# Hybrid decoder layer: raw output weights in token places, norm weights loaded in the last block, output tile and probabilities in pools by use, row diagonals ahead of sums

## The chip, the core and the metric

The kernel runs on one core of one Trainium2 chip. What is measured is the device time of one execution in microseconds. Before the change three runs took 1560.19, 1560.9 and 1562.3 us, a median of 1560.9. The program is written in Bass and Tile: each engine (TensorE or PE, VectorE or DVE, ScalarE or ACT, GpSimd or POOL, SyncE or SP, which issues most DMAs) has its own queue of instructions and works it off in order; semaphores tie the queues together.

## The reference

One step of a decoder layer on 4096 new prompt tokens and 64 sampled tokens, all in float32. `h @ w_in` is one projection to 2816 columns; three groups of heads use its columns, and their outputs go through one output projection:

```python
h = _rmsnorm(x, g_pre)
z = h @ w_in
cb, cc, ch, cg, q, k, v, ag, mq, mg = _split_cols(z)
...
out_a = jax.nn.silu(cg) * cb * conv                      # gated short convolution
o_b = _window_prompt(q, k, v, sink_g)                    # window of 128, 8 query heads, 2 key heads, sinks
out_b = jax.nn.silu(ag) * o_b
o_c = _mem_attend(mq.reshape(n, t, MEM_HEADS, HEAD_DIM), mem_k, mem_v)   # 4 heads over 256 memory tokens
out_c = jax.nn.silu(mg) * o_c
y = jnp.concatenate([out_a, out_b, out_c], axis=-1) @ w_out
return x + _rmsnorm(y, g_post), new_conv, new_k, new_v
```

The sampled tokens attend to cached keys and values instead. Besides the two outputs, the new keys, values and convolution states are returned.

## The kernel before

**Two halves.** The first half (`input_projection` and, for its first two blocks of tokens, `plain_block`) computes z for 8 blocks of 520 tokens each. It does so in three phases (`PHASES`), each for a part of the columns. Inside a phase, a block is made in seven products (`PRODUCTS`; a step is one product, `p` = 0 to 6) after Strassen's scheme, each in float32 as three passes over a high and a low part: `split` and `w_split` copy a tensor to its rounded high part on ACT and subtract to get the low part on DVE. The second half, attention and the output projection, runs over 33 blocks of 128 tokens (`Block`) and over 16 chunks of 256 tokens (`Chunk`).

**The last block of the third phase** (`ph == 2`, `b == last`) also prepares the second half: during its steps `wo_load` brings the 16 raw tiles of the output weights, 128x512 each (j = 0 to 15; j below 8 is the first half of the output columns), and `wo_split` splits each two steps later into a tile of the pool "wa". The raw tiles are taken from the pool "work" (tag "u"), which has five buffers: the sixth raw tile waits until the first has been split. "wa" has 21 buffers, which in this phase hold the weights of the seven products; each becomes free when its product is done. "hx" holds the four x tiles of the products; the last x is loaded three steps ahead, so its places become free during the last steps. When the last block is done, its z parts are split into zh and a remainder (`finish_parts`, L400 and L402) and stored to the DRAM tensor qd.

**The opening of attention.** `open_attention` closes the pools of the first half and opens those of the second in the same memory; a new tile that lies over an old one has to wait for the old one's last reader. Before the change, pool "wp" has the window probabilities (tags "sm", "pt", "pv"), "xp" those of the memory heads ("p", "xpt"), and "yp" on the other side holds the input rows xr, the output tile yn and one mix buffer. Then chunk 1's gates are loaded (`load_mix`), the rows of blocks 0 and 1 (`Block.load`), and `gpost`, the norm weights, 512 KB as one row broadcast over 128 partitions. All of these are issued by SP, in this order, behind the stores to qd.

**The units.** A chunk has eight units: four of window attention and four of memory attention. `window_unit` makes scores on PE (L1205), copies half of them from PSUM (ACT, L1207), replaces masked ones by the other half (DVE, L1208), takes maxima and exponentials and normalises; later it transposes (PE, L1228) and masks (POOL, L1235 and L1238). `cross_unit` is alike, with L1141, L1145, L1150 (POOL) and L1156. Scores of all units share two PSUM banks, transposes another two. `Pipe` starts a unit at given places of the output products (L1432): eight in each of the first two blocks, which therefore carry a whole chunk each, four in each later block. So while block 0's output is computed, chunk 1's units run. `Block.run` multiplies each half of the output by gpost (L1439), squares it (L1440), and adds the row (L1450). `Block.split` (L1412, L1413) splits the mixed heads of the next block.

**The order of instructions.** The first phase is written out by hand (`plain_jobs` and a manual schedule). From the second phase on a scheduler orders each engine's queue by estimated times, with a few instructions pinned by `keep_in_program_order`; so a change of a buffer or of a load's place also changes the order of what follows.

**The row factors.** RMSNorm of x needs a factor for each token. For block 2 of the first phase `rows_diag` writes five diagonal tiles of 104x104 (DVE, L291), `rows_product` multiplies them with ones (PE, L300), which spreads the factors over all partitions. `plain_jobs` lists in which step of which block this and the sums of weights (`first_sums`) are done.

Of the kernel before, what the change touches and what calls it, by code (L numbers as in the profile page):

```python
# [8 lines left out]
F32 = mybir.dt.float32  # L9
# [3 lines left out]
ALU = mybir.AluOpType  # L13
# [38 lines left out]
def hybrid_layer(ctx: ExitStack, tc: tile.TileContext, a: dict):  # L52
# [240 lines left out]
    def rows_bank(b):  # L293
        rows[b] = accumulator(1, 2, f"rows_y{b}")[:, :, :HW]
# [322 lines left out]
    def plain_jobs(b, s):  # L617

        gains = lambda b, *os: [lambda o=o: x_gain(0, b, o) for o in os]
        scales = lambda b, *os: [lambda o=o: x_scale(0, b, o) for o in os]  # L620
        parts = lambda b, o: [lambda: x_split(b, o)]
        fill = lambda o: [lambda q=q: first_fill(o, q) for q in range(4)]
        sums = lambda q, k: [lambda: first_sums(q, k)]
        fills = lambda q, *os: [lambda o=o: first_fills(q, o) for o in os]
        done = lambda b, row: finish(0, b, zz[b], row)
        row = [row_step]
        return {
            (0, 0): lambda: [*fill("A11"), *parts(0, "B21")],
            (0, 1): lambda: fill("A22"),
            (0, 2): lambda: [*fill("A12"), *parts(0, "B12"), *row],  # L630
            (0, 3): lambda: [*sums(0, 0), *row, *sums(0, 1), *fills(0, "S2"), *row],
            (0, 4): lambda: [*parts(0, "B22"), *fills(0, "S3", "S1"), *row, *fills(0, "S4"), *row],
            (0, 5): lambda: [*sums(1, 0), *row, *sums(1, 1), *fills(1, "S2", "S3"), *row],
            (0, 6): lambda: [*parts(1, "B11"), *row, *fills(1, "S1", "S4"), *sums(3, 0), *row],
            (0, 7): lambda: [*row, *fills(3, "S2", "S3"), lambda: rows_diag()],
            (1, 0): lambda: [*parts(1, "B21"), *row, *row, lambda: rows_bank(0), lambda: rows_product(0), *z_rows(0, 1)],
            (1, 1): lambda: [*z_rows(0, 0), *done(0, 1), *row, *row],
            (1, 2): lambda: [*parts(1, "B12"), *done(0, 0), *fills(3, "S1"), *row],
            (1, 3): lambda: sums(2, 0),
            (1, 4): lambda: [*row, *parts(1, "B22"), *gains(2, "B11"), *sums(2, 1), lambda: rows_diag(), lambda: rows_bank(2),  # L640
                             *fills(2, "S2"), *row],
            (1, 5): lambda: [lambda: rows_product(2), *fills(2, "S3", "S1"), *gains(2, "B21"), *fills(2, "S4"), *row],
            (1, 6): lambda: [*scales(2, "B11"), *gains(2, "B12"), *scales(2, "B21", "B12"), *row],
            (1, 7): lambda: [lambda: h_split(0), *gains(2, "B22"), *scales(2, "B22"), lambda: t_sum(0, 2, "T1"), *row,
                             *z_rows(1, 1)],
        }[b, s]()
# [220 lines left out]
    def wo_load(j):  # L867
        h, k = divmod(j, KT)
        wo_raw[j] = third["work"].tile([P, 512], F32, tag="u", name=f"wor{j}")
        DMA.dma_start(wo_raw[j], a["w_out"][k][:, 512 * h : 512 * h + 512])  # L870

    def wo_split(j):
# [12 lines left out]
              (1, 0, 4): lambda: next_fills("S4"),  # L885
              (1, 0, 5): lambda: next_fills("A22")}

    def input_projection():
        for i, (ph, b, p) in enumerate(steps):
# [36 lines left out]
            if ph == 2 and b == last:  # L926
                for j in ((0, 1, 2), (3, 4), (5, 6, 7), (8, 9), (10, 11, 12), (13, 14, 15), ())[p]:
                    jobs.append(lambda j=j: wo_load(j))
                    pending.setdefault(i + 2, []).append(lambda j=j: wo_split(j))
                if p == 4:  # L930
                    jobs.append(blocks[0].split)
# [35 lines left out]
    def open_attention():  # L967

        nonlocal ps, mixp, wp, xp, vp, bp, bq, yp
        own.close()  # L970
# [8 lines left out]
        bq = att.enter_context(tc.tile_pool(name="bq", bufs=1))  # L979
        wp = att.enter_context(tc.tile_pool(name="wp", bufs=2))  # L980
        xp = att.enter_context(tc.tile_pool(name="xp", bufs=2))
        bp = att.enter_context(tc.tile_pool(name="bp", bufs=1))
# [6 lines left out]

    ps = mixp = wp = xp = vp = bp = bq = yp = None  # L990
    att = ctx.enter_context(ExitStack())
# [8 lines left out]

    def work(pool, shape, tag, name, **kw):

        if ps is None:
            return third["work"].tile(shape, F32, tag="u", name=name)
        return pool.tile(shape, F32, tag=tag, name=name, **kw)

# [42 lines left out]
    class Chunk:  # L1049
# [83 lines left out]
        def cross_unit(self, h, pts):  # L1133
            c, nb = self.c, CT // P
            q = self.q[:, h]
            p = work(xp, [P, nb, 256], "p", f"xp{c}_{h}")
            mx, nm, den, rd = (tiny.tile([P, 4], F32, tag=n, name=f"x{n}{c}_{h}") for n in ("mx", "nm", "den", "rd"))
# [13 lines left out]
            yield 1  # L1151
            pt = work(xp, [P, 2, CT], "xpt", f"xpt{c}_{h}")
            for kt in range(2):
# [42 lines left out]
        def window_unit(self, i, kvh, steps):  # L1196
            b = 2 * self.c + i
            first = b == 0
            sm = work(wp, [P, 4, P], "sm", f"sm{b}_{kvh}")
            for half in range(2):  # L1200
# [26 lines left out]
            for hh in range(4):  # L1227
                TE.transpose(t[:, hh * P : (hh + 1) * P], sm[:, hh, :], ident)  # L1228
            pt = work(wp, [P, 512], "pt", f"wpt{b}_{kvh}")
            S.copy(pt, t)  # L1230
            p3 = pt.rearrange("p (h q) -> p h q", h=4)
            if not first:

                pv = work(wp, [P, 512], "pv", f"wpv{b}_{kvh}")
# [78 lines left out]
    def sample_window():  # L1313
# [20 lines left out]
        transpose_to(vn, [(zs[:, 5, :], 64)], "svnt")  # L1334
        sms = [wp.tile([P, 4, P], F32, tag="sm", name=f"ssm{half}").rearrange("p a n -> p (a n)")[:, : 2 * 192] for half in range(2)]
        sms = [t.rearrange("p (a n) -> p a n", a=2) for t in sms]
# [28 lines left out]
        yield  # L1365
        pt = wp.tile([P, 512], F32, tag="pt", name="swpt")
        transpose_to(pt, [(sm[i][:, 0:P], P) for i in range(4)], "swt0")
        ptn = wp.tile([P, 512], F32, tag="pv", name="swptn")[:64]
        transpose_to(ptn, [(sm[i][:, P:192], 64) for i in range(4)], "swt1")
# [19 lines left out]
    class Block:  # L1389
# [70 lines left out]
    blocks[1].load()  # L1460
    gpost = wa.tile([P, 2, 512], F32, tag="w", name="gpost").rearrange("p a n -> p (a n)")
    DMA.dma_start(gpost, a["gpost"].partition_broadcast(P))

# [158 lines left out]
```

## Time and profile before

| | us |
|---|---|
| median of three runs | 1560.9 |
| profiled execution, whole | 1560.18 |
| its span, from the first to the last instruction | 1558.4 |
| PE busy in the span | 1538.1 |
| mean granted PE clock | 0.996 of full |
| scores of chunk 1's first window unit on PE | from 941.6 |

A row of a timeline has the start and the length in us, the engine, the line of the kernel, the operation, the tiles as out<-in with the shape, and the number of instructions; brackets give how long the engine had been idle before it and what ended the wait. SPq is the queue of SP, which only issues DMAs; the length is that of the issue and not of the transfer. Matmuls overlap their neighbours by their pipeline, so a row's length is more than the step from one to the next. In the table of stages each engine has its busy time and its number of instructions, then comes the granted share of PE's clock, the mean busy share of the 16 DMA engines and the rate in GB/s.

### The profile page before, as it was taken

The page shows a single profiled execution, that of the slowest core. Times are in us where ns is not written, and L with a number is a line of the kernel's source. Part 1 is how long each engine was busy: PE and PEld are TensorE (multiplying, and loading weights), DVE is VectorE, ACT ScalarE, POOL GpSimd, SP SyncE. Part 2 cuts the span into 40 slices and gives each one's busy share as a digit, 9 for nine tenths or more (in the row PEclk, how much of TensorE's full clock was granted, in tenths as well). Part 3 has the DMA queues.
Part 4 walks back from the last instruction along what each step waited for, and adds up shares of the span by engine and source line. Part 5 has one row for each costly group of instructions (what it writes and reads, how often), then busy time and mean ns, then how long its engine had stood idle before and what let it go on. Part 6 is the DMA issues. An engine that isn't in the chain of part 4 may idle for free.

```text
span 1558.4 us, 30165 instructions
## 1 busy us (share of the span) xinstructions
PE 1538.1 (99%) x11341; PEld 1411.4 (91%) x11341; DVE 1155.2 (74%) x2075; ACT 796.3 (51%) x2031; POOL 380.7 (24%) x603
## 2 busy tenths in 40 slices
PE   9999999999999999999999998999999999999998
PEld 9999999999999999999999996788888888887876
DVE  6779888898988777986777677776666666666643
ACT  6776566575222222445454355666655655655632
POOL 0323232211300000010012103544444444444310
PEclk9999999999999999999999999999999999999999
DMA  9979999877755333679666969888777777777332
GB/s 265 199 206 260 249 277 269 291 237 259 191 178 178 124 124 124 245 225 311 231 223 196 278 219 279 166 171 157 164 149 159 146 147 158 152 160 154 122 109 95
DMA packets 175110, 305.59 MB, mean 196 GB/s; under 512 B 31093, under 2 KB 104821, under 8 KB 174933
## 3 DMA queue, kind: packets, MB, share of 16 engines
q1 hardware_dynamic: 128069, 226.69, 47.0%
q0 software_dynamic: 46176, 75.92, 25.5%
q8 instruction: 90, 1.47, 0.4%
q10 hardware_dynamic: 720, 1.05, 0.2%
q14 instruction: 55, 0.45, 0.1%
HBM read 196.54 MB, written 108.05 MB: 195 GB/s over the span
## 4 chain that ended last, share of the span: by engine, by line
PE 86%; DVE 4%; DMA 4%; issue 3%; ACT 1%; POOL 1%; SPq 0%; DVEq 0%; ACTq 0%; POOLq 0%
PE c L359 48%; PE y L1432 22%; PE ws L1205 3%; PE wo L1047 2%; PE wt L1228 2%; PE xs L1141 2%; PE xt L1156 2%; PE wo L1177 2%; PE wo L1183 1%; PE mem_acc L772 1%; DMA gpost<-in_gpost 1%; DMA wor<-in_w_out 1%; DMA vd<-v 0%; DVE z L366 0%; DMA rb<-rowd 0%
## 5 line engine op out<-in xcount | busy, mean ns | idle before, releaser
L1432 PE MATMUL y<-wo,mh 128*128 128x512 f32 (+1 forms) x1040 | 350.3, 400 | 0.0
L366 DVE TENSOR_TENSOR z<-c,z 128x520 f32<-128x520 f32 (+1 forms) x308 | 194.7, 645 | 90.8 <-PE c L359 89.5
L1432 PEld LDWEIGHTS y<-wo,mh 128*128 128x128 f32 x1040 | 194.3, 188 | 38.8 <-issue 2.0
L1432 PE MATMUL y<-wo,ml 128*128 128x512 f32 (+1 forms) x520 | 201.9, 388 | 0.0
L1218 ACT ACTIVATE sm<-sm,wnm 128x128 f32<-128x128 f32 x256 | 99.6, 391 | 70.7 <-DVE wnm L1212 70.7
L1150 POOL TENSOR_SCALAR xp<-xp,xrd 128x256 f32<-128x256 f32 x128 | 74.6, 589 | 192.2 <-DVE xrd L1146 192.1
L1432 PEld LDWEIGHTS y<-wo,ml 128*128 128x128 f32 x520 | 98.3, 189 | 16.2
L1142 DVE TENSOR_REDUCE xmx<-xs 128x2 f32<-128x512 f32 x64 | 44.1, 689 | 58.3 <-PE xs L1141 58.2
L1230 ACT COPY wpt<-wt 128x512 f32<-128x512 f32 x64 | 37.2, 582 | 86.2 <-PE wt L1228 86.2
L1205 PEld LDWEIGHTS ws<-kst,q 128*128 128x128 f32 x512 | 70.9, 193 | 10.2 <-issue 5.3
L1205 PE MATMUL ws<-kst,q 128*128 128x256 f32 x512 | 73.6, 285 | 4.9 <-issue 4.9
L1439 DVE TENSOR_TENSOR yn<-y,gpost 128x512 f32<-128x512 f32 (+1 forms) x66 | 45.1, 683 | 40.3 <-PE y L1432 39.2
L1440 ACT ACTIVATE y<-y 128x512 f32<-128x512 f32 (+1 forms) x66 | 38.5, 584 | 64.9 <-DVE yn L1439 64.9
L730 POOL CAST wmask<-negs 128x256 uint8<-128x256 f32 x1 | 1.4, 1372 | 267.9 <-DMA negs<-in_wmask 267.9
L1080 POOL DMA_DIRECT2D q<-qd x64 | 42.9, 676 | 97.4 <-DVE lo_7T L350 65.3
L1238 POOL TENSOR_SCALAR_AFFINE_SELECT wpt<-wpt 128x512 f32<-128x512 f32 x64 | 54.2, 848 | 48.3 <-ACT wpt L1230 45.4
L1145 ACT ACTIVATE xp<-xs,xnm 128x256 f32<-128x256 f32 x128 | 58.9, 464 | 4.4 <-DVE xnm L1143 4.2
L1069 POOL DMA_DIRECT2D kst<-qd x64 | 38.6, 619 | 83.1 <-PE xt L1156 42.0
L1235 POOL TENSOR_SCALAR_AFFINE_SELECT wpv<-wpt 128x512 f32<-128x512 f32 x62 | 40.4, 652 | 65.3 <-ACT wpt L1230 65.0
L1208 DVE COPY_PREDICATED sm<-wmask,ws 128x256 f32<-128x256 uint8 x124 | 52.3, 435 | 2.8 <-ACT sm L1207 2.6
L1450 DVE SCALAR_TENSOR_TENSOR xr<-yn,yst,xr 128x1024 f32<-128x1024 f32 (+2 forms) x34 | 43.5, 1282 | 13.5 <-POOL yst L1446 13.5
L1207 ACT COPY sm<-ws 128x256 f32<-128x256 f32 x128 | 44.8, 367 | 13.0 <-PE ws L1205 6.6
(962 smaller groups left out, 5119.5 us busy)
## 6 DMA issues: line engine op xcount, KB each, us to landing
q<-qd POOLq DMA_DIRECT2D x64, 384.0 KB, 7.7
xr<-in_x_p SPq DMA_DIRECT2D x32, 512.0 KB
nat<-in_x_p SPq DMA_DIRECT2D x39, 416.0 KB
o_yp<-xr SPq DMA_DIRECT2D x31, 512.0 KB
md<-th POOLq DMA_DIRECT2D x48, 260.0 KB, 6.5
qd<-zh SPq DMA_DIRECT2D x48, 260.0 KB
qd<-z SPq DMA_DIRECT2D x48, 260.0 KB
kst<-qd POOLq DMA_DIRECT2D x60, 192.0 KB, 5.8
```

Of the source, the lines that this page charges most:

```text
L359: TE.matmul(bank[:, :HW], l, r, start=first and i == 0, stop=last and i == 3 * KH - 1)
L366: add = lambda dst, other: V.tensor_tensor(dst, c, other, op=ALU.add)
L1142: V.tensor_reduce(mx[:, :nb], s, axis=AX.X, op=ALU.max)
L1145: S.activation(p[:, i, :], s[:, i, :], AF.Exp, bias=nm[:, i : i + 1], scale=SCALE, accum_out=den[:, i : i + 1])
L1150: G.tensor_scalar(p[:, i, :], p[:, i, :], rd[:, i : i + 1], 0.5, op0=ALU.mult, op1=ALU.mult)
L1205: TE.matmul(s3[:, hh, :], self.q[:, 4 + 2 * (2 * half + hh) + kvh, i * P : i * P + P], self.kst[:, 2 * kvh + part, i * P : i * P + 2 * P], ...
L1207: S.copy(sm[:, 2 * half : 2 * half + 2, :], s3[:, :, P : 2 * P])
L1208: V.copy_predicated(sm[:, 2 * half : 2 * half + 2, :], third["wmask"], third["negs"] if first else s3[:, :, 0:P])
L1218: S.activation(sm[:, hh, :], sm[:, hh, :], AF.Exp, bias=nm[:, hh : hh + 1], scale=SCALE, accum_out=den[:, hh : hh + 1])
L1238: G.affine_select(p3, p3, pattern=[[0, 4], [1, P]], compare_op=ALU.is_ge, fill=0.0, base=0, channel_multiplier=-1)
L1432: TE.matmul(acc, self.hl[l][:, k], wo[k][c0 // 512][:, r, c0 % 512 : c0 % 512 + c1 - c0], start=j == 0, stop=j == passes * KT - 1)
L1439: V.tensor_tensor(yn[:m, c0:c1], acc[:m], gpost[:m, c0:c1], op=ALU.mult)
```

## The change

Five things are done. Raw weights 10 to 13 go into two places of "hx", two to a place, and the loads of 10, 11 and 13 to 15 are issued one step earlier (the splits of 10 to 12 stay in the last step, p = 6, those of 13 to 15 move into it). `gpost` is loaded in step p = 2 of the last block, in a tile of "wa" as before. The probabilities and the output tile yn get a pool for each use ("sm", "p", "yn", "pt", "pv", "xpt"), all on the left side, with as many buffers as before; yn leaves "yp". In `plain_jobs` (1, 4), `rows_diag` and `rows_bank` come ahead of the split of B22, the gains and the second sum of weights. The instruction that negates the sink column of the sampled tokens is kept in program order.

```diff
-            (1, 4): lambda: [*row, *parts(1, "B22"), *gains(2, "B11"), *sums(2, 1), lambda: rows_diag(), lambda: rows_bank(2),
+            (1, 4): lambda: [*row, lambda: rows_diag(), lambda: rows_bank(2), *parts(1, "B22"), *gains(2, "B11"), *sums(2, 1),
                              *fills(2, "S2"), *row],
...
     def wo_load(j):
         h, k = divmod(j, KT)
-        wo_raw[j] = third["work"].tile([P, 512], F32, tag="u", name=f"wor{j}")
+        if 10 <= j < 14:
+
+            if j % 2 == 0:
+                third["raw"] = hxp.tile([P, KH, HW], F32, tag="hx", name=f"wor{j}").rearrange("p k n -> p (k n)")
+            wo_raw[j] = third["raw"][:, 512 * (j % 2) : 512 * (j % 2) + 512]
+        else:
+            wo_raw[j] = third["work"].tile([P, 512], F32, tag="u", name=f"wor{j}")
         DMA.dma_start(wo_raw[j], a["w_out"][k][:, 512 * h : 512 * h + 512])
...
+    def gains_load():
+        third["gpost"] = wa.tile([P, 2, 512], F32, tag="w", name="gpost").rearrange("p a n -> p (a n)")
+        DMA.dma_start(third["gpost"], a["gpost"].partition_broadcast(P))
...
-                for j in ((0, 1, 2), (3, 4), (5, 6, 7), (8, 9), (10, 11, 12), (13, 14, 15), ())[p]:
+                for j in ((0, 1, 2), (3, 4), (5, 6, 7), (8, 9, 10, 11), (12, 13, 14, 15), (), ())[p]:
                     jobs.append(lambda j=j: wo_load(j))
-                    pending.setdefault(i + 2, []).append(lambda j=j: wo_split(j))
+                    pending.setdefault(i + (3 if j in (10, 11) else 2), []).append(lambda j=j: wo_split(j))
+                if p == 1:
+                    pending.setdefault(i + 1, []).append(gains_load)
...
-        wp = att.enter_context(tc.tile_pool(name="wp", bufs=2))
-        xp = att.enter_context(tc.tile_pool(name="xp", bufs=2))
+        places = {tag: att.enter_context(tc.tile_pool(name=tag, bufs=1 if tag == "yn" else 2))
+                  for tag in ("sm", "p", "yn", "pt", "pv", "xpt")}
...
-    def work(pool, shape, tag, name, **kw):
+    def work(shape, tag, name):
 
         if ps is None:
             return third["work"].tile(shape, F32, tag="u", name=name)
-        return pool.tile(shape, F32, tag=tag, name=name, **kw)
+        return places[tag].tile(shape, F32, tag=tag, name=name)
...
-        V.tensor_scalar(scol[:, 1:2], scol[:, 0:1], -1.0, None, op0=ALU.mult)
+        tc.keep_in_program_order(V.tensor_scalar(scol[:, 1:2], scol[:, 0:1], -1.0, None, op0=ALU.mult))
...
-            yn = yp.tile([P, D], F32, tag="yn", name=f"yn{b}", bufs=1)
+            yn = work([P, D], "yn", f"yn{b}")
...
-    gpost = wa.tile([P, 2, 512], F32, tag="w", name="gpost").rearrange("p a n -> p (a n)")
-    DMA.dma_start(gpost, a["gpost"].partition_broadcast(P))
+    gpost = third["gpost"]
```

The other edits replace `work(wp, ...)`, `work(xp, ...)` and `wp.tile(...)` by `work(...)` with the tag.

More of the change, by code (lines that the diff above doesn't have):

```diff
@@ L967, in open_attention @@
     def open_attention():
-        nonlocal ps, mixp, wp, xp, vp, bp, bq, yp
+        nonlocal ps, mixp, places, vp, bp, bq, yp
         own.close()
@@ L988, in open_attention @@
         DMA.dma_start(third["scol"][:, 0:1], a["sinkcol"])
-    ps = mixp = wp = xp = vp = bp = bq = yp = None
+    ps = mixp = places = vp = bp = bq = yp = None
     att = ctx.enter_context(ExitStack())
@@ L1135, in cross_unit @@
             q = self.q[:, h]
-            p = work(xp, [P, nb, 256], "p", f"xp{c}_{h}")
+            p = work([P, nb, 256], "p", f"xp{c}_{h}")
             mx, nm, den, rd = (tiny.tile([P, 4], F32, tag=n, name=f"x{n}{c}_{h}") for n in ("mx", "nm", "den", "rd"))
@@ L1151, in cross_unit @@
             yield 1
-            pt = work(xp, [P, 2, CT], "xpt", f"xpt{c}_{h}")
+            pt = work([P, 2, CT], "xpt", f"xpt{c}_{h}")
             for kt in range(2):
@@ L1198, in window_unit @@
             first = b == 0
-            sm = work(wp, [P, 4, P], "sm", f"sm{b}_{kvh}")
+            sm = work([P, 4, P], "sm", f"sm{b}_{kvh}")
             for half in range(2):
@@ L1228, in window_unit @@
                 TE.transpose(t[:, hh * P : (hh + 1) * P], sm[:, hh, :], ident)
-            pt = work(wp, [P, 512], "pt", f"wpt{b}_{kvh}")
+            pt = work([P, 512], "pt", f"wpt{b}_{kvh}")
             S.copy(pt, t)
@@ L1232, in window_unit @@
             if not first:
-                pv = work(wp, [P, 512], "pv", f"wpv{b}_{kvh}")
+                pv = work([P, 512], "pv", f"wpv{b}_{kvh}")
                 G.affine_select(pv.rearrange("p (h q) -> p h q", h=4), p3, pattern=[[0, 4], [-1, P]], compare_op=ALU.is_gt,
@@ L1334, in sample_window @@
         transpose_to(vn, [(zs[:, 5, :], 64)], "svnt")
-        sms = [wp.tile([P, 4, P], F32, tag="sm", name=f"ssm{half}").rearrange("p a n -> p (a n)")[:, : 2 * 192] for half in range(2)]
+        sms = [work([P, 4, P], "sm", f"ssm{half}").rearrange("p a n -> p (a n)")[:, : 2 * 192] for half in range(2)]
         sms = [t.rearrange("p (a n) -> p a n", a=2) for t in sms]
@@ L1365, in sample_window @@
         yield
-        pt = wp.tile([P, 512], F32, tag="pt", name="swpt")
+        pt = work([P, 512], "pt", "swpt")
         transpose_to(pt, [(sm[i][:, 0:P], P) for i in range(4)], "swt0")
-        ptn = wp.tile([P, 512], F32, tag="pv", name="swptn")[:64]
+        ptn = work([P, 512], "pv", "swptn")[:64]
         transpose_to(ptn, [(sm[i][:, P:192], 64) for i in range(4)], "swt1")
```

## The prediction

> **What bounds the kernel now.** I read the page's busy times first, then the busy time by stage, then the timelines of the one stage that stands out. The page says TensorE:
>
> ```profile
> PE 1538.1 (99%) x11341; PEld 1411.4 (91%) x11341; DVE 1155.2 (74%) x2075; ACT 796.3 (51%) x2031; POOL 380.7 (24%) x603
> ```
>
> So at most 1558.4 - 1538.1 = 20.3 us of the span can be PE idling, and only a change to PE's idle time or to its clock can matter. The busy time by stage (start:end, then length, PE, PEld, DVE, ACT, POOL, granted PE clock, DMA share, GB/s) shows where. The projection ends and attention begins at about 941:
>
> ```profile
> 930.00:940.00 10.00, 10.00 (x86) 10.00 (x85) 10.00 (x16) 7.79 (x13) 2.56 (x4) 1.00 0.42 115
> 940.00:950.00 10.00, 8.44 (x48) 7.09 (x47) 5.26 (x9) 3.40 (x8) 0.08 (x1) 1.00 1.41 292
> 950.00:960.00 10.00, 6.61 (x30) 5.86 (x31) 8.10 (x22) 5.03 (x23) 1.60 (x3) 0.83 0.91 312
> 960.00:970.00 10.00, 8.43 (x54) 6.52 (x52) 6.94 (x18) 7.57 (x28) 8.69 (x16) 1.00 1.16 332
> 970.00:980.00 10.00, 8.94 (x47) 5.88 (x47) 6.21 (x20) 6.34 (x25) 2.13 (x5) 0.66 1.30 275
> 980.00:990.00 10.00, 9.60 (x66) 6.51 (x65) 8.23 (x23) 6.37 (x27) 5.27 (x9) 1.00 1.30 252
> 990.00:1000.00 10.00, 9.19 (x63) 7.75 (x64) 7.93 (x19) 7.03 (x25) 7.41 (x12) 1.00 0.41 103
> 1100.00:1200.00 100.00, 100.00 (x614) 82.06 (x613) 68.71 (x175) 58.85 (x220) 45.42 (x71) 1.00 0.76 155
> ```
>
> Before and after this passage PE is full; inside it PE idles and, in two slices, runs at a lower clock. PE's timeline names the gaps, in brackets with their releaser:
>
> ```profile
> 953.39 2.04 PE L1205 MATMUL ws<-kst,q 128*128 128x256 f32 x8 [4.95 <-issue]
> ...
> 968.52 0.98 PE L1156 MATMUL xt<-ident,xp 128*128 128x128 f32 x4 [1.30 <-issue]
> 971.14 1.54 PE L1047 MATMUL wo<-xpt,mkv 128*64 128x256 f32 x5 [1.06 <-DVE xpt L1160]
> ...
> 983.92 0.63 PE L1156 MATMUL xt<-ident,xp 128*128 128x128 f32 x4 [0.40 <-DVE xpt L1160]
> 993.00 0.33 PE L1156 MATMUL xt<-ident,xp 128*128 128x128 f32 x1 [0.81 <-POOL xp L1150]
> 998.24 0.63 PE L1141 MATMUL xs<-mk,q 128*128 128x256 f32 x4
> ```
>
> Idle: 4.95 + 1.30 + 1.06 + 0.40 + 0.81 = 8.5 us. Clock: 10 x (1 - 0.83) + 10 x (1 - 0.66) = 5.1 us of PE work not done. Together 13.6 us: **the ceiling** for anything done to this passage. The last row is my mark: from the scores at 998.24 on, the instructions stand in the same order on every compute engine in both programs (but for one of 128x1), so whatever is gained by then stays, and nothing later changes.
>
> **Why PE stops at 948.** The score product at 953.39 needs a PSUM bank that DVE must first read (the predicated copy, L1208, behind ACT's copy, L1207). The queues of SP, POOL, ACT and DVE in turn:
>
> ```profile
> 931.80 0.93 SPq L870 DMA_DIRECT2D wor<-in_w_out  x2
> 934.22 0.33 SPq L870 DMA_DIRECT2D wor<-in_w_out  x1
> 939.92 0.48 SPq L870 DMA_DIRECT2D wor<-in_w_out  x1
> ...
> 937.45 2.64 POOL L1080 DMA_DIRECT2D q<-qd  x4 [65.29 <-DVE lo_7T L350]
> ...
> 936.76 0.62 ACT L178 CAST wo<-wor 128x512 fp32r<-128x512 f32 x1 [0.44 <-DMA wor<-in_w_out]
> 947.54 0.62 ACT L178 CAST wo<-wor 128x512 fp32r<-128x512 f32 x1 [3.12 <-DMA wor<-in_w_out]
> 949.77 0.62 ACT L178 CAST wo<-wor 128x512 fp32r<-128x512 f32 x1 [0.28 <-DMA wor<-in_w_out]
> ...
> 948.20 0.69 DVE L182 TENSOR_TENSOR wo<-wor,wo 128x512 fp32r<-128x512 f32 x1 [3.58 <-ACT wo L178]
> 950.42 0.69 DVE L182 TENSOR_TENSOR wo<-wor,wo 128x512 fp32r<-128x512 f32 x1 [1.52 <-ACT wo L178]
> 951.03 1.91 DVE L402 TENSOR_TENSOR z<-z,zh 128x520 fp32r<-128x520 f32 x3
> 952.86 0.77 DVE L1208 COPY_PREDICATED sm<-wmask,ws 128x256 f32<-128x256 uint8 x2
> ```
>
> The raw weights rotate through five tiles, so the last (j = 15) is issued only at 939.92, once an earlier one has been split; by then POOL has put four query loads on the DMA engines (share 0.42 before, 1.41 after). It lands 949.77 - 939.92 = 9.85 us later, while the one of 934.22 took 936.76 - 934.22 = 2.54. ACT and DVE keep order, so its split holds up the predicated copy.
>
> **The change, part by part.** (1) *Raw weights 10 to 13 in "hx" places.* Weights 14 and 15 then take the tiles of 5 and 6, which today go to 10 and 11 at 931.80: the last issue moves from 939.92 to about 932.7. The query loads for chunk 2 lie over those hx places and so must now wait for the splits of 10 to 13: they can no longer run ahead of the weights. The last landing is bounded by 932.7 + 2.54 = 935.3 and 932.7 + 9.85 = 942.6; I take the first, since the DMA share there is 0.42. ACT then does all eight casts without a wait. For DVE, today's work up to the first predicated copy holds waits of 3.58 + 1.52; against that the new order puts the residue of block 1's mix (L1413, 1.22, row below) in front: 952.86 - 5.10 + 1.22 = **948.98**. Score unit 1 then has its bank at about 949.4 instead of 953.3. PE's first output half ends at 953.39 - 4.95 = 948.4 in both, and in the new order six products of the second half stand ahead of the scores, at 2.77 / 12 = 0.23 each (row below) 1.4 us: 949.8. So the 4.95 goes, and with it the 1.7 us of low clock behind it.
>
> ```profile
> 1004.61 2.77 PE y L1432 x12
> ```
>
> (2) *gpost in the last block.* Today its load stands behind loads that wait for the last stores to qd:
>
> ```profile
> 957.62 0.38 SPq L1089 DMA_DIRECT2D mix<-md  x1
> 959.30 0.73 SPq L1462 DMA_DIRECT2D gpost<-in_gpost  x1
> ...
> 955.02 0.45 DVE L1208 COPY_PREDICATED sm<-wmask,ws 128x256 f32<-128x256 uint8 x1 [0.68 <-ACT sm L1207]
> 967.39 1.22 DVE L1413 TENSOR_TENSOR ml<-place,mh 128x1024 fp32r<-128x1024 f32 x1
> 969.93 0.69 DVE L1439 TENSOR_TENSOR yn<-y,gpost 128x512 f32<-128x512 f32 x1 [0.92 <-DMA gpost<-in_gpost]
> 970.67 0.42 DVE L1160 COPY xpt<-xt 128x256 f32<-128x256 f32 x1
> ...
> 975.97 0.69 DVE L1186 TENSOR_TENSOR mix<-mix,wo 128x512 f32<-128x512 f32 x1 [1.73 <-PE wo L1183]
> 978.04 0.17 DVE L1146 RECIPROCAL xrd<-xden 128x2 f32<-128x2 f32 x1 [1.05 <-ACT xp L1145]
> 979.12 0.21 DVE L1445 TENSOR_SCALAR yst<-yst 128x1 f32<-128x1 f32 x1 [0.91 <-ACT y L1440]
> ```
>
> It moves to just ahead of weight 5, so ahead of the 931.80 of today's weight 10, and is first used after 948.98: over 17 us. At twice a weight's bytes it needs between 2.54 and 10.6 us (today's 959.30 to 969.93), both inside the 17. On SP it passes only weights 5 to 15, which have the time of (1); its slot in "wa" is free by then, and the total of 21 slots is unchanged. Gone is the wait of 0.92, and the mix loads and stores behind it are issued sooner, since the stores follow L402.
>
> (3) *What that does to the rest of the passage.* From DVE's first predicated copy (952.86) to the mark (998.24) are 45.4 us. In it the 1.22 of L1413 is already done and the 0.92 is gone. At 975.97 and 978.04 DVE waits 1.73 and 1.05 for products of PE's slow stretch (the second through ACT's exponentials), 2.8 us that go if PE keeps its clock; at 955.02 another 0.68 goes in the same way; the 0.91 at 979.12 waits for ACT's square and stays. 45.4 - 1.2 - 0.9 - 2.8 - 0.7 = 39.8; from 948.98 the mark comes at 988.8, or 989.5 without the last term. I take 989.0: **gain 9.2 us**, which leaves 13.6 - 9.2 = 4.4 us of PE's loss, about one low-clock stretch (1.7) and 2.7 of idling. Bounds: if the passage keeps its present density after the earlier start, 952.86 - 948.98 = 3.9 us; if no loss is left, 13.6. The value is nearer the middle because DVE, busy 8.23 of 10 in its best-filled slice here, will not fill up fully: each of the first two blocks carries a whole chunk, the later ones half of one.
>
> PE's clock went low at 970 although the longest gap just before was 1.30, and the 4.4 goes by that. [...]
>
> (4) *Pools by use.* No tile has fewer buffers. The first yn now lies over hi of the projection's last product, which PE has read before 948.4; the first xpt over stored halves of z, read by the first stores of all. Today the first yn is written at 969.93 and xpt beside it, long after both: cost 0, bounded either way by the 1.30 of the gap at the transposes that fill xpt. (5) *Row diagonals ahead of sums.*
>
> ```profile
> 75.92 8.98 PE c L359 x75
> 84.91 0.94 PE rows_y L300 x4
> 85.84 12.99 PE c L359 x108
> ...
> 83.95 1.00 DVE L291 TENSOR_SCALAR mix_s<-ident,r 104x104 f32<-104x104 f32 x5
> ```
>
> In the chain of waits PE goes from c to rows_y to c without a gap, though the diagonals end only at 84.95: nothing to win. DVE's split of B22 and the two sums come 1.00 later, hidden by the 13 us of products. Bounded either way by one of the five writes, 1.00 / 5 = 0.2; I take 0. The scale of scol moves behind all this: one instruction of 128x1, 0.
>
> **Sum.** The profiled execution took 1560.18 us (span 1558.4 and 1.8 around it); 1560.18 - 9.2 = 1551.0. Its time is 0.7 below the runs' median of 1560.9; from the median it is 1551.7. I say 1551.5.
>
> **Rivals.** *A. Only the first stall goes* (gain 3.1 to 7; mid 5.3, 1555.6). DVE and ACT become the bound of the two dense blocks: DVE is at 8.23 even where PE is at 9.60, and the new PE order spends the output products early, so that fewer are left as filler around score units. For it: the 3.9 of the unchanged density. Against: several of DVE's waits are PE's low clock. *B. Nearly all goes* (gain 12 to 13.6; mid 12.8, 1548.1): needs PE to stay at full clock and DVE to fill up. [...] *C. It doesn't do what it says* (within 3.1 of before, 1560.9): the removed waits come back at the stores; POOL's key load for chunk 2 now waits for all halves of z stored, and its normalising (L1150, 0.81 at 993) stands behind it in order. *D. Slower.* ACT now casts all eight weights before it makes the halves zh. If the last lands late all the same, everything stands behind it: 949.77 + 0.62 + 0.69 for its split, six L402 at 1.91 / 3 and L1413's 1.22 give 956.1 for the predicated copy against 952.86. That is 3.3 more, a second low-clock stretch 1.7, less 0.9 for gpost: 1560.9 + 4.1 = 1565.0. It decides from a landing at 949.77 - 3.3 = 946.5. For it: gpost adds bytes ahead of the weights. Against: an issue at 932.7 with a share of 0.42 would have to take 13.8 us, and the longest seen is 9.85.
>
> **How the numbers follow.** Forecast (gain 7 to 12) 0.60, A 0.19, B 0.08, C 0.06, D 0.07. The likeliest one's own range is 1548.9 to 1553.9. The range from 1547.3 (the ceiling) to 1557 (the 3.9 of the unchanged density) leaves out C, D and the edge of A. A measurement of this kernel tells 0.2%, 3.1 us, from no change: faster 0.87, same 0.06, slower 0.07.
>
> **What would show it.** (1) Right if no ACT cast of a weight waits for its load after 940, DVE's first predicated copy starts at 948 to 950, and PE has no gap over 1 us before 955. (2) Right if no row waits for gpost. (3) Right if the chunk-2 scores that stand at 998.24 start at 987 to 991; the rest must be shifted by the same amount. (5) Right if the products of 85.84 start at the same time. Wrong if the query loads still overlap the last weights, if the mix load of 957.62 is issued no earlier, or if the low clock lasts as long as today (10 us).

## The result and the profile after

| | before | after |
|---|---|---|
| median of 7 runs each | 1562.3 us (1560.19 to 1567.64) | 1554.16 us (1549.46 to 1556.89) |
| ratio after to before | | 0.9942, 95% interval 0.9921 to 0.9962 |
| profiled execution | 1560.18 us, span 1558.4 | 1554.59 us, span 1552.9 |
| second set (e9 and e10, on one chip), 12 + 23 and 6 runs | 1560.95 and 1561.97 us | 1553.41 us, ratio 0.9950 (0.9937 to 0.9963) |

The kernel is faster by 0.5 to 0.6%, some 8 to 9 us. The busy time by stage of the changed kernel, with the columns of the prediction (start:end, length, PE, PEld, DVE, ACT, POOL, PE clock, DMA share, GB/s):

```profile
930.00:940.00 10.00, 10.00 (x85) 10.00 (x85) 9.18 (x14) 7.91 (x13) 0.00 (x0) 1.00 0.63 223
940.00:950.00 10.00, 10.00 (x66) 9.11 (x65) 10.00 (x19) 5.96 (x11) 2.64 (x4) 1.00 0.67 178
950.00:960.00 10.00, 10.00 (x58) 8.45 (x57) 8.67 (x25) 7.28 (x33) 0.12 (x1) 1.00 1.28 338
960.00:970.00 10.00, 6.70 (x36) 5.33 (x36) 4.27 (x12) 4.69 (x20) 9.05 (x17) 0.83 1.12 302
970.00:980.00 10.00, 10.00 (x71) 7.46 (x71) 9.05 (x26) 7.33 (x30) 6.36 (x12) 1.00 1.29 281
980.00:990.00 10.00, 9.81 (x64) 6.80 (x64) 7.92 (x23) 8.63 (x33) 6.36 (x10) 1.00 1.59 255
990.00:1000.00 10.00, 10.00 (x71) 7.95 (x71) 7.37 (x23) 6.75 (x28) 5.20 (x10) 1.00 0.58 127
```

PE is full from 940 to 960, where it idled before, and has one hole left, at 960 to 970, with the only low clock of the passage. In that slice POOL is the fullest engine (9.05 of 10 us). PE's timeline of the changed kernel names the hole; the last row is the mark:

```profile
963.43 0.44 PE L1168 MATMUL xt<-ident,xp 128*128 128x128 f32 x2 [2.71 <-POOL xp L1162]
...
965.04 0.48 PE L1168 MATMUL xt<-ident,xp 128*128 128x128 f32 x1 [0.59 <-POOL xp L1162]
...
993.06 0.63 PE L1153 MATMUL xs<-mk,q 128*128 128x256 f32 x4
```

Rows of the other engines' timelines, SP, POOL, ACT and DVE in turn:

```profile
925.50 9.59 SPq L876 DMA_DIRECT2D wor<-in_w_out  x11
...
949.70 0.67 SPq L165 DMA_DIRECT2D qd<-zh  x1
950.46 0.40 SPq L165 DMA_DIRECT2D qd<-z  x1
...
944.96 2.64 POOL L1092 DMA_DIRECT2D q<-qd  x4 [70.44 <-DVE wo L182]
959.88 2.38 POOL L1081 DMA_DIRECT2D kst<-qd  x4 [12.28 <-DMA sneg<-in_smask]
962.22 0.69 POOL L1247 TENSOR_SCALAR_AFFINE_SELECT wpv<-wpt 128x512 f32<-128x512 f32 x1
962.85 0.52 POOL L1162 TENSOR_SCALAR xp<-xp,xrd 128x256 f32<-128x256 f32 x1
...
936.51 3.97 ACT L178 CAST wo<-wor 128x512 fp32r<-128x512 f32 x7
941.31 0.62 ACT L178 CAST wo<-wor 128x512 fp32r<-128x512 f32 x1 [0.30 <-PE c L359]
...
950.93 0.77 DVE L1220 COPY_PREDICATED sm<-wmask,ws 128x256 f32<-128x256 uint8 x2
951.59 0.68 DVE L1451 TENSOR_TENSOR yn<-y,gpost 128x512 f32<-128x512 f32 x1
958.46 0.16 DVE L1158 RECIPROCAL xrd<-xden 128x2 f32<-128x2 f32 x1
```

The weights are issued in one run on SP and cast without a wait for a load. DVE multiplies the first output half by `gpost` at 951.59, where the kernel before did so at 969.93. But POOL stands at chunk 2's keys until 959.88. The tile of that load lies over high halves (zh) of the last block, so in the compiled program it waits for seven stores to qd, of which SP issued the last, `qd<-zh`, at 949.70. The trace has this store landed at 959.12, and the keys start 0.76 us after that; in the kernel before the same store landed at 957.61, and the keys start 0.79 us later, at 958.40. The reciprocal for the first normalising (L1162) is there at 958.46 + 0.16; the normalising starts at 962.85, behind the keys and one select, and PE waits for it.

**A measure finer than the whole time.** The trace lists 11,341 matmuls in every kernel here. I call the time from the start of the 7,501st (still projection) to that of the 8,251st (an output product past the passage) *the stretch*. In all fourteen traces 505.1 to 505.2 us lie between its end and the start of the last matmul, so what differs is the stretch and what comes before. The time from the first to the 1,001st matmul, where every kernel but for the order in step (1, 4) has the same work, varies by 5 us from one execution to the next:

| kernel | first 1,000 matmuls | stretch | against before |
|---|---|---|---|
| before (profile above; e9; e5 as a third) | 125.1; 124.8; 125.4 | 126.34; 124.04; 126.54, mean 125.6 | |
| after (profile above; e10; e8 as a third) | 126.9; 125.0; 125.4 | 118.37; 118.08; 118.06, mean 118.2 | -7.4 |
| e1 weights only | 127.7 | 121.50 | -4.1 |
| e2 places of the weights only | 129.5 | 120.50 | -5.1 |
| e6 gpost only | 126.6 | 121.14 | -4.5 |
| e3 all but the weights | 127.2 | 120.97 | -4.7 |
| e7 all, but yn in its old place | 124.3 | 121.87 | -3.8 |
| e12 before, keys by SP | 127.0 | 120.48 | -5.1 |
| e4, e11 after, keys by SP | 124.4; 126.9 | 115.30; 115.18 | -10.4 |

(e5 and e8 stand as repeats because the stretch shows no effect of their edits.) Each of three single edits (the weights, gpost, the keys) is worth 4 to 5 us in the stretch, and they do not add up. The three traces of before scatter by 2.5 us and most other kernels have one trace, so a figure of the last column is good to a us or two. The experiments say why the edits do not add up. Line numbers in them are a few lower or higher than in the changed kernel.

### The profile page after: what moved, and what is told of

It reads as the page before. It is cut to its first block, busy times and chain, and to the rows that moved or that the text cites. A ratio compares the mean times of both kernels' runs of the same rounds, so it can differ in the third digit from the quotient of the medians.

```text
span 1552.9 us, 30171 instructions
## 1 busy us (share of the span) xinstructions
PE 1535.6 (99%) x11341; PEld 1410.3 (91%) x11341; DVE 1152.5 (74%) x2075; ACT 796.1 (51%) x2031; POOL 381.5 (25%) x603
## 4 chain that ended last, share of the span: by engine, by line
PE 82%; DMA 7%; DVE 5%; issue 3%; ACT 1%; POOL 1%; SPq 1%; DVEq 0%; POOLq 0%; ACTq 0%
PE c L359 43%; PE y L1444 22%; PE ws L1217 4%; PE wo L1059 2%; PE wt L1240 2%; PE xs L1153 2%; PE xt L1168 2%; PE wo L1189 2%; DMA place<-in_xt 2%; DMA nat<-in_x_p 1%; PE wo L1195 1%; DMA wr_3A<-in_w_in 1%; PE mem_acc L772 1%; DMA md<-th 1%; DMA qd<-z 1%
## 5 line engine op out<-in xcount | busy, mean ns | idle before, releaser
L1162 POOL TENSOR_SCALAR xp<-xp,xrd 128x256 f32<-128x256 f32 x128 | 75.5, 597 | 197.2 <-DVE xrd L1158 197.2
L1250 POOL TENSOR_SCALAR_AFFINE_SELECT wpt<-wpt 128x512 f32<-128x512 f32 x64 | 54.3, 848 | 48.4 <-ACT wpt L1242 45.4
L1462 DVE SCALAR_TENSOR_TENSOR xr<-yn,yst,xr 128x1024 f32<-128x1024 f32 (+2 forms) x34 | 43.0, 1268 | 13.6 <-POOL yst L1458 13.6
L272 ACT ACTIVATE nat<-nat 104x1024 f32<-104x1024 f32 x40 | 42.2, 1055 | 20.8 <-DMA nat<-in_x_p 20.8
```

The source lines that it names most:

```text
L1162: G.tensor_scalar(p[:, i, :], p[:, i, :], rd[:, i : i + 1], 0.5, op0=ALU.mult, op1=ALU.mult)
L1250: G.affine_select(p3, p3, pattern=[[0, 4], [1, P]], compare_op=ALU.is_ge, fill=0.0, base=0, channel_multiplier=-1)
L1462: V.scalar_tensor_tensor(self.xr[:m, cs], yn[:m, cs], st[:m, 3:4], self.xr[:m, cs], op0=ALU.mult, op1=ALU.add)
```

## The experiments

**e1, the weights alone.** The kernel before with

```diff
-        wo_raw[j] = third["work"].tile([P, 512], F32, tag="u", name=f"wor{j}")
+        if 10 <= j < 14:
+            if j % 2 == 0:
+                third["raw"] = hxp.tile([P, KH, HW], F32, tag="hx", name=f"wor{j}").rearrange("p k n -> p (k n)")
...
-                for j in ((0, 1, 2), (3, 4), (5, 6, 7), (8, 9), (10, 11, 12), (13, 14, 15), ())[p]:
+                for j in ((0, 1, 2), (3, 4), (5, 6, 7), (8, 9, 10, 11), (12, 13, 14, 15), (), ())[p]:
```

> The kernel before with the raw output weights alone changed: 10 to 13 in the token places, and the new order of loads and splits; gpost, the pools and the diagonals are as before. Theory F (the weights carry the whole gain): 0.992 to 0.996 of before, some 9 us, as the changed kernel has; no gap of 4.95 us on TensorE ahead of the first window scores of the last passage, and DVE may wait about 0.9 us for gpost near 958 without any wait of TensorE behind it. Rival G (gpost, pools or diagonals carry a part): at most 6 us of gain, ratio 0.9965 or more.

Measured: ratio 0.9987 (0.9974 to 1.0001), stretch 121.50. Theory F fell. The 4.95 us gap ahead of the window scores is gone, but one nearly as long (4.28) stands some products later. DVE's and PE's timelines of this kernel:

```profile
960.91 0.69 DVE L1445 TENSOR_TENSOR yn<-y,gpost 128x512 f32<-128x512 f32 x1 [4.54 <-issue]
...
962.30 0.91 PE L1234 MATMUL wt<-ident,sm 128*128 128x128 f32 x4 [4.28 <-issue]
```

DVE stands 4.54 us at the first output product and the window transposes wait behind it. `gpost` isn't what is late: SP's row for it here is at 941.54,

```profile
941.54 0.33 SPq L1468 DMA_DIRECT2D gpost<-in_gpost  x1
```

19 us earlier. The profile puts the wait down to "issue"; in the compiled program this product waits for six stores to qd and one POOL instruction. The last of these stores was issued at 951.83 and landed at 960.63, 0.28 us before the product starts. Its tile, yn, lies at bytes 180,896 to 184,992 of each partition, across two halves of z (177,376 to 181,536 and 181,536 to 183,616). In the changed kernel yn lies at 139,616, and the product waits for PE alone.

**e2, the places without the order.** Only the first hunk of e1's edit.

> The kernel before with raw weights 10 to 13 in the token places, but loaded in the steps and split in the steps of before. Theory Q (the wait for a free raw place is what holds the last loads): the loads no longer wait for a split, so they are issued some us earlier and at least 6 of the 9 us come. Rival R (the steps in which the loads and splits stand hold them, and the query loads that now wait for the splits of 10 to 13 come later still): at most 3 us of gain, and the ACT casts of the last weights stand behind the last splits of z or beyond.

Measured: ratio 0.9966 (0.9953 to 0.9978), stretch 120.50, 5.1 us shorter: less than the 6 that theory Q set, well over R's 3. SP issues the eleven last weights in one run, as in the changed kernel:

```profile
927.31 10.19 SPq L876 DMA_DIRECT2D wor<-in_w_out  x11
```

So it was the wait for a free raw place that held the loads, and the new order of loads adds nothing that the stretch shows.

**e3, everything but the weights.** The changed kernel with e1's edit taken back.

> The changed kernel with the raw weights as before in places and order: what is left is gpost loaded in the last block, the pools by use, the diagonals ahead of the sums and scol in program order. Theory F (these four cost and bring nothing): 0.998 to 1.002 of before, the 4.95 us gap and the stretch at half clock are there again. Rival G: 0.9965 or less, or above 1.002 if the pools add a wait.

Measured: ratio 0.9958 (0.9943 to 0.9973), stretch 120.97. Theory F fell a second time. The first gap is there as foretold, but the later ones (1.30 and 1.06) are not, and only the clock after the first gap is low. PE's timeline, then the busy time by stage:

```profile
956.73 2.05 PE L1211 MATMUL ws<-kst,q 128*128 128x256 f32 x8 [4.85 <-issue]
```

```profile
950.00:960.00 10.00, 5.15 (x21) 4.23 (x20) 7.47 (x15) 5.74 (x17) 0.00 (x0) 0.72 1.09 377
960.00:970.00 10.00, 10.00 (x63) 8.58 (x61) 7.25 (x22) 8.02 (x34) 6.67 (x13) 0.94 0.99 282
970.00:980.00 10.00, 9.97 (x69) 7.32 (x68) 7.97 (x26) 7.22 (x32) 7.82 (x14) 1.00 1.25 288
```

**e4, the keys on SyncE.** PE's last hole in the changed kernel stands behind POOL's key load; here SP issues it.

```diff
-                    G.dma_start(self.kst[half * 64 : half * 64 + 64, 2 * kvh : 2 * kvh + 2, lo:],
-                                  qd[:, 0, kvh * 64 : kvh * 64 + 64, t0 - P + lo : t0 + CT].rearrange("a p n -> p a n"))
+                    dst = self.kst[half * 64 : half * 64 + 64, 2 * kvh : 2 * kvh + 2, lo:]
+                    src = qd[:, 0, kvh * 64 : kvh * 64 + 64, t0 - P + lo : t0 + CT].rearrange("a p n -> p a n")
+                    if c == 2:
+                        DMA.dma_start(f(dst), f(src))
+                    else:
+                        G.dma_start(dst, src)
```

> The changed kernel with the four loads of chunk 2's keys issued by SyncE instead of GpSimd, the rest as it is. In the changed kernel these loads stand on GpSimd at 959.88 for 2.38 us, ahead of the normalising of the cross scores (L1162), and TensorE waits 2.71 and 0.59 us for it. Theory K (the loads, which wait for the last stores of z, hold GpSimd): GpSimd normalises at about 958.6 to 960, both gaps fall under 1 us in sum, and so does the stretch at half clock of 3.41 us: 3 to 5 us less than the changed kernel, ratio to before 0.990 to 0.993. Rival L (ScalarE's and VectorE's chain sets the time of the normalising, GpSimd would wait for them anyway): within 1.5 us of the changed kernel, and the gap at 960.7 keeps 1.5 us or more.

Measured: ratio 0.9933 (0.9915 to 0.9952), stretch 115.30, 2.9 us under the changed kernel's. POOL's timeline, then the busy time by stage:

```profile
956.90 0.93 POOL L1166 TENSOR_SCALAR xp<-xp,xrd 128x256 f32<-128x256 f32 x2 [11.11 <-DVE xrd L1162]
```

```profile
950.00:960.00 10.00, 10.00 (x65) 8.62 (x63) 8.23 (x26) 8.99 (x38) 3.03 (x7) 1.00 1.08 322
960.00:970.00 10.00, 8.97 (x63) 6.24 (x62) 8.52 (x25) 6.34 (x29) 7.38 (x12) 1.00 1.17 335
```

POOL now waits for the reciprocal, not for stores; the clock stays at 1.00 in every slice. Theory K holds in its mechanism: the hole was POOL's wait. The 2.9 us are just short of the 3 to 5 that it gave, because two new waits come in (below).

**e5 and e6, the two small edits apart.** e5 is the kernel before with the pools by use alone, e6 the kernel before with `gains_load` alone:

```diff
+                if p == 1:
+                    pending.setdefault(i + 1, []).append(gains_load)
...
-    gpost = wa.tile([P, 2, 512], F32, tag="w", name="gpost").rearrange("p a n -> p (a n)")
-    DMA.dma_start(gpost, a["gpost"].partition_broadcast(P))
+    gpost = third["gpost"]
```

> The kernel before with the pools by use alone. Theory Z (two locks on the first output product of block 0, yn<-y,gpost on DVE: it needs gpost, and its tile lies over z halves whose stores must have landed; either alone keeps it late in DVE's order): with the tile moved off z but gpost still loaded after the last stores, the product stays at its late place in DVE's order, the passage from 940 to 1000 is within 1 us of before, ratio 0.998 to 1.002. Rival G (the pools carry the 5 us by themselves): passage 3 us or more shorter, ratio 0.998 or less.

> The kernel before with gpost alone loaded early in the last block. Theory Z: the product's tile still lies over z halves, it moves up in DVE's order and then waits there for their stores, DVE stands; the passage gains at most 2 us or loses, ratio 0.998 to 1.003. Rival H (gpost's landing, 0.92 us of DVE's wait in the kernel before, was the only lock): the passage is about 5 us shorter, ratio 0.9975 or less.

Measured: e5 1.0004 (0.9995 to 1.0012), stretch 126.54; e6 0.9983 (0.9974 to 0.9992), stretch 121.14. Theory Z holds for the pools alone. For gpost alone it is wrong and rival H right as to the stretch, though the whole time moved by 2.7 us where H asked for 3.9. DVE's product in e5 and then in e6:

```profile
971.75 0.69 DVE L1439 TENSOR_TENSOR yn<-y,gpost 128x512 f32<-128x512 f32 x1 [1.41 <-DMA gpost<-in_gpost]
```

```profile
961.81 0.69 DVE L1445 TENSOR_TENSOR yn<-y,gpost 128x512 f32<-128x512 f32 x1
```

In e6 the product comes 10 us earlier and waits for nothing, although its tile still lies over z: with the weights late, DVE gets to it only when the stores have landed (the last at 960.08). In e1 it got there at 956.4 (960.91 - 4.54) and had to wait.

**e7, one tile put back.** The changed kernel with

```diff
-            yn = work([P, D], "yn", f"yn{b}")
+            yn = yp.tile([P, D], F32, tag="yn", name=f"yn{b}", bufs=1)
```

> The changed kernel with one tile, yn, back in the pool of before, over the z halves; weights, gpost, the other pools and the diagonals stay changed. Theory Z: DVE waits 3 to 5 us at the first product yn<-y,gpost for stores that land at about 960, TensorE's window transposes wait behind it, and the time is 2 to 5 us above the changed kernel's, ratio to before 0.9955 to 0.9985. Rival K (GpSimd's wait with chunk 2's keys sets the passage, DVE's wait lies beside it): within 1 us of the changed kernel, 0.993 to 0.995.

Measured: ratio 0.9969 (0.9956 to 0.9981), stretch 121.87, 3.7 us more than the changed kernel's. DVE and PE:

```profile
957.00 0.69 DVE L1451 TENSOR_TENSOR yn<-y,gpost 128x512 f32<-128x512 f32 x1 [4.14 <-issue]
...
958.39 0.74 PE L1240 MATMUL wt<-ident,sm 128*128 128x128 f32 x4 [3.89 <-issue]
```

Theory Z holds in its mechanism: `gpost` had long been loaded, the last store that the product waits for landed at 956.73, and DVE starts at 957.00. By the stretch the place of this one tile is worth 3.7 us. By the whole time it is less sure: the medians of e7 and of e8 below (the changed kernel but for the diagonals), run on one chip, are 1554.77 and 1553.6, and the intervals of their ratios overlap. (Without yn's pool the tiles behind it also lie 4,096 bytes lower and the rows xr lie where they did before; the wait of 4.14 us is yn's own, for the six stores as in e1.)

**e8, the old order of the diagonals.** The changed kernel with the (1, 4) list of before.

> The changed kernel with the diagonals and the row bank behind the weight sums of step (1, 4) again, as before. Forecast (no cost, no gain): within 0.1% of the changed kernel, ratio to before 0.993 to 0.9955. Rival J (in runs whose loads land late, the row copies then reach TensorE late): the stage from 64 to 95 us loses 2 us more than in runs of the changed kernel, and the median is 1 to 3 us above it, 0.995 to 0.9965.

Measured: ratio 0.9958 (0.9944 to 0.9971), stretch 118.06; the changed kernel had 0.9942 and 0.9950. No effect on the stretch, as it should be. The edit acts among the first 1,000 matmuls: the six traces with the new order have 124.3 to 127.2 us there, the eight with the old one 124.8 to 129.5. The means, 125.8 and 126.4, differ by less than either scatters. The place itself says more. In four of the eight traces with the old order PE stands 0.99 to 2.45 us ahead of the row product while DVE still writes the diagonals (e6, e1, e12, e2), with the new order in one of six (0.94, e3). PE's timeline of e2:

```profile
87.57 2.07 PE L300 MATMUL rows_y<-mix_s,ones 104*128 104x260 f32 x4 [2.45 <-DVE mix_s L291]
```

In e2 the old order has 1.68 + 0.68 + 0.69 = 3.05 us of DVE's work (the split and two additions for the sums) between the rest and the diagonals; with the new order, in e3, it stands behind them. What the new order brings in the whole time stays open.

**e9 and e10, both kernels once more; e11 and e12, the keys again.** e11 is e4, beside the changed kernel on one chip; e12 is the kernel before with e4's edit.

> The kernel before once more, unchanged, to see what two sets of runs of one kernel differ by and whether its passage from 940 to 1000 repeats. If the passage is the same in every execution and the spread of the times comes from the first 95 us: gaps on TensorE of 4.9 to 5.4, 1.6 and 1.4 to 1.9 us and clocks near 0.83 and 0.66 in the same places, passage within 0.5 us of the first profile, ratio 0.999 to 1.001. If the passage itself varies: other gaps, 2 us or more off.

> The changed kernel once more, as the measure for the next one on the same chip: passage 7.5 to 8.5 us shorter than before's, ratio 0.993 to 0.9965, with the gap of about 2.7 us ahead of the cross transposes (L1168) again.

> The changed kernel with chunk 2's keys issued by SyncE, once more, beside the changed kernel on the same chip. Theory K: passage about 11 us shorter than before's and 3 us shorter than the changed kernel's, median 1.5 to 4 us under the changed kernel's. Rival: what separated the two in the first profile was the early loads alone; then the medians lie within 1 us.

> The kernel before with chunk 2's keys issued by SyncE and nothing else. Theory K says that GpSimd's wait decides only where the weights and the output product no longer come later (in the kernel before GpSimd is back at 960.8, ahead of the normalising): passage within 1 us of before's, ratio 0.999 to 1.001. Rival: the keys hold the passage in the kernel before too, 2 us or more shorter, 0.9985 or less.

Measured: e9 0.9996 (0.9982 to 1.0009), e10 0.9950, e11 0.9934 (0.9920 to 0.9947), e12 0.9970 (0.9957 to 0.9984). e10 and e11 repeat their stretches within 0.3 us; on the same chip their medians are 1553.41 and 1551.46, the stretches 2.9 us apart. e11 is the best version here, ahead of both kernels, though the two intervals of the ratios overlap.

e9 missed: the stretch came out 2.3 us shorter than in the first profile. Its gaps are the old ones but for one (0.44 for 1.06); the clock differs:

```profile
950.00:960.00 10.00, 6.52 (x27) 5.96 (x27) 7.76 (x21) 4.64 (x21) 1.39 (x3) 0.66 0.89 308
960.00:970.00 10.00, 8.43 (x55) 6.90 (x53) 7.30 (x19) 7.70 (x29) 8.04 (x15) 1.00 1.15 335
970.00:980.00 10.00, 9.56 (x66) 6.92 (x67) 8.33 (x24) 8.27 (x33) 5.43 (x11) 1.00 1.30 278
```

e9 has two units of low clock, of 3.41 us each, at the first gap and none at 970; the first profile had one at the first gap and two at 970. In a unit the granted clock is 0.50, and in the first profile two products of L1432 start 0.43 us apart there, against the 0.23 of the prediction's row at 1004.61:

```profile
955.23 0.63 PE L1432 MATMUL y<-wo,ml 128*128 128x512 f32 x1
955.66 1.04 PE L1432 MATMUL y<-wo,mh 128*128 128x512 f32 x2
```

So one unit costs up to 3.41 x 0.50 = 1.7 us by the clock's share, less where PE idles in it: e9's low clock starts at 951.63, 1.85 us before the gap ends.

e12 missed too: I had said that the keys decide only once the other waits are gone, and alone they bring 5.1 us. POOL's rows of e12 and of the kernel before say how:

```profile
962.99 0.93 POOL L1154 TENSOR_SCALAR xp<-xp,xrd 128x256 f32<-128x256 f32 x2 [21.14 <-DVE scol L1332]
963.88 0.62 POOL L1239 TENSOR_SCALAR_AFFINE_SELECT wpv<-wpt 128x512 f32<-128x512 f32 x1
```

```profile
961.33 0.64 POOL L1235 TENSOR_SCALAR_AFFINE_SELECT wpv<-wpt 128x512 f32<-128x512 f32 x1 [0.55 <-ACT wpt L1230]
962.72 0.63 POOL L1235 TENSOR_SCALAR_AFFINE_SELECT wpv<-wpt 128x512 f32<-128x512 f32 x1 [0.76 <-ACT wpt L1230]
963.31 1.22 POOL L1238 TENSOR_SCALAR_AFFINE_SELECT wpt<-wpt 128x512 f32<-128x512 f32 x2
964.52 1.83 POOL L1150 TENSOR_SCALAR xp<-xp,xrd 128x256 f32<-128x256 f32 x4
```

With the key loads gone from POOL, the first two normalisings stand ahead of the selects; in the kernel before all four stand behind four selects, 1.5 us later. e12 changes the planner's order on POOL, and the 1.30 and 1.06 at PE are gone in its trace. (That the planner does so because it takes POOL to be free earlier is my reading.)

**What stays open.** For e1 and e6 the stretch is 4.1 and 4.5 us shorter, the whole time by its ratio only 2.0 and 2.7. One profile stands for each, and the part ahead of the stretch scatters by 5 us; I can't say from these runs where the difference lies. For e3 it is the other way round: 4.7 by the stretch, 6.6 by the ratio.

## Why the prediction was right, and where it was not

The time, the direction and the passage were right: 1554.16 lies in the range, 2.7 over the 1551.5. The shares within the sum were not.

- **(1) The weights.** Right in its mechanism. The last weights are issued by 925.50 + 9.59 = 935.1, no cast waits for a load after 940, the first predicated copy starts at 950.93. The changed kernel's profile runs 2.4 us late ahead of the passage (7,501st matmul at 922.82 against 920.45 before), so the 948.98 should be read as 951.3: off by 0.4. PE has no gap until 960, and the query loads come only at 944.96, behind the weights. e2 shows that the free place does it.
- **(2) gpost.** Mis-sized. The prediction counted the wait of 0.92 that stood in the profile, and e6 measures 4.5 us. A wait shows only what is left after the planner has set a late product late in DVE's order; loaded early, the product moved from 969.93 to 961.81, and PE's gaps of 1.30 and 1.06 went with their low clock (one of 1.64 behind POOL came in). Against e9 alone, which lacked the low clock at 970, the 4.5 would be 2.9. In the changed kernel no row waits for gpost, as foretold, and the first mix load comes at 959.14, or at 956.7 less the 2.4, against 957.62.
- **(3) The rest of the passage.** Right in kind, short by 2.1 us. From the first predicated copy to the mark the forecast had 989.0 - 948.98 = 40.0; the profile has 993.06 - 950.93 = 42.1 and before it was 45.4. By the stretch the two profiles differ by 126.34 - 118.37 = 8.0, so that 13.6 - 8.0 = 5.6 of PE's loss are left where the forecast had 4.4 without a place for them. Of these, 2.71 + 0.59 of idling and 1.7 of low clock are POOL's wait: rival C's mechanism, to which the prediction gave the whole gain as its price and 0.06 as its chance. It came beside the forecast, at a part of that price. C's text says that the key load waits for the stores only now; in the kernel before it already waited for five of them, and the last to land was the same one, at 957.61. New is that the first reciprocal is ready earlier (958.62, against 961.04 in the kernel before, where POOL was done with the keys at 960.78), so the normalising now meets the wait. e4 takes all 5.0 away and wins 2.9; two waits of 1.03 and 1.20 come in their place (rows at the end).
- **(4) Pools at 0: the step that failed.** "Today the first yn is written at 969.93 [...] long after both: cost 0" measured the new place by the old time of the write. Steps (1) and (2) of the same prediction moved that write 18 us forward, to 951.59. There the old place isn't free, and the new one is: e7 puts a price of 3.7 us on it by the stretch, e5 one of nothing where the rest is as before. Without yn's new place the weights and gpost (with the other pools, e7, -3.8) bring no more than either alone.
- **(5) Diagonals and scol at 0.** Not contradicted by the times; e8 can't tell a small effect from the scatter. But "nothing to win" was read from the one profile at hand, in which PE happened not to wait; four of eight traces with the old order show a wait of 0.99 to 2.45 there.
- **The mark** at 993.06, less the 2.4, is 990.7, and 990.90 in e10: inside the 987 to 991 given, at its late end. The rest moved by the same amount: 505.1 us lie between the stretch and the last matmul in both kernels.
- **The clock.** The prediction went by the row at 970, where the longest gap just before was 1.30, and took one low unit as left: there is one, from 964.65 to 968.06 (0.83 in its slice), behind 2.71 of idling.

So the total came out near for a wrong reason: of the 7.4 us that the stretch shows, the two edits that carried the sum of 9.2 bring 3.8 without yn's new place, and the edit that was costed at nothing brings the other 3.6. That the sum of terms so far off came near the measured time is luck.

## What to carry to other kernels

A wait in a profile prices an edit only while everything around it stays: where a planner sets the order, a late operand shows up as a late place in the queue more than as a wait. For each edit that you cost at nothing, move its instructions to the times that your other edits give them, and look again at what their memory was used for; places over buffers whose stores still run are taken until the stores land (the product started 0.28 us after the last landing in e1, 0.27 in e7). And test edits together, not only alone: here the weights and gpost, 4.1 and 4.5 us by themselves, made 3.8 with each other while yn kept its old place, and the pools, worth nothing alone, raised that to 7.4.

## What the runs showed of the hardware

In the clock records of the two profiles of before and after, the low clock of the passage is 0.50 of full and lasts 3.41 us, or 6.83, two such units in a row: one unit at the first gap of before (953.14 to 956.55), two at 970 (970.20 to 977.03), one in the changed kernel (964.65 to 968.06). Gaps of like length stand beside one unit or beside two: 4.95 us of idling beside one in the first profile of before (0.83 in its slice), 5.11 beside two in e9 (951.63 to 958.46; 0.66 above). Shorter gaps differ as well: 2.36 and 0.60 us stand beside one unit in e10 (0.83 from 960 to 970), and 1.30 with 1.06 beside the two at 970 in the kernel before (0.66), while 1.31 with 0.44 (e9), and 1.03 and 1.20 some 15 us apart (e4), stand beside none (1.00 in their slices):

```profile
961.21 0.44 PE L1168 MATMUL xt<-ident,xp 128*128 128x128 f32 x2 [2.36 <-POOL xp L1162]
962.83 0.48 PE L1168 MATMUL xt<-ident,xp 128*128 128x128 f32 x1 [0.60 <-POOL xp L1162]
```

```profile
969.40 0.98 PE L1156 MATMUL xt<-ident,xp 128*128 128x128 f32 x4 [1.31 <-issue]
971.40 0.86 PE L1047 MATMUL wo<-xpt,mkv 128*64 128x256 f32 x5 [0.44 <-DVE xpt L1160]
```

```profile
968.07 0.71 PE L1221 MATMUL ws<-kst,q 128*128 128x256 f32 x4 [1.03 <-DMA kst<-qd]
...
983.60 0.33 PE L1172 MATMUL xt<-ident,xp 128*128 128x128 f32 x1 [1.20 <-POOL xp L1166]
```

In the kernel before and in e10 the low clock starts at 970.20 and 962.56, inside the second of the two gaps. Which gaps bring a low unit, and whether one or two, these runs don't settle.
